# A decoder layer's delta rule and attention: one hop per unit of weights, substitution over both token tiles, bias loaded a step ahead

## The chip, the cores and the metric

One core of one Trainium2 chip runs the whole program. The metric is the device time of one execution in microseconds; the median of three runs is compared. A profile is one further execution, recorded by the hardware profiler.

## The reference, cut to what matters

One decoder layer over 256 tokens of width 2048, in fp32. After an RMS norm, one projection feeds two branches of 8 heads of 128: a gated delta rule (convolution over 4 tokens, chunks with a triangular solve, a state carried from chunk to chunk) and block attention with a relative position bias (256 tokens are one block, so it is plain causal attention). Both are gated, merged and projected; then a SwiGLU network of width 5632.

```python
u = rmsnorm(h); q_a,k_a,v_a,z_a,beta_a,dec_a,q_b,k_b,v_b,gate_a,gate_b = split(u @ w_in)
# delta rule, per head and chunk; L strictly lower triangular
wu = triangular_solve(eye + L, [k*beta*exp(g), v*beta])
v_new = u - w @ S;  o = q_dec @ S + A @ v_new;  S = S*exp(g_last) + k_dec.T @ v_new
y_a = rmsnorm(o, o_norm_w) * silu(z_a)
# attention
y_b = softmax(q_b @ k_b.T * scale + rel_bias, causal) @ v_b
h = h + (sigmoid(gate_a)*(y_a @ w_a) + sigmoid(gate_b)*(y_b @ w_b)) @ w_out
h = h + (silu(u @ w_gate) * (u @ w_up)) @ w_down,  u = rmsnorm(h)
```

## The kernel before, in words

All weights come as 503 *units* of 128x1024 fp32 (512 KB), loaded in order by SP (`Weights.load`, up to 7 raw buffers). ScalarE rounds each to a high part `whi` (line 64), VectorE subtracts to get the low part `wlo` (line 65), up to three units ahead, in 4 buffers each. TensorE multiplies each unit with the activations, themselves split into high and low: `fm_jobs` (lines 156 and 157, 16 matmuls a unit, feature-major output) and `tm_job` (lines 177 to 179, 12 matmuls of 512 columns a unit, token-major output).

Everything else is laid between these units. A *hop* is one call of `tick()`: it runs what stands in `late` (convolution taps, transposes of finished tiles), then goes on with the first generator of `chains` until its next `yield`. `fm_jobs` and `tm_job` call it once for every two units. When a generator ends, the next begins in the same hop. `drain()` ticks without any unit between. The generators are `x_scale` and `beta_decay` (norm of the input, gates of the delta rule; they run beside the first group's projections), `gdn(g)` for two groups of four heads, and `moba(g)` for two groups of heads. `gdn(0)` begins with the second group's convolved projections (24 feature-major units, then 8 for `z`), `gdn(1)` and the `moba`s run beside the attention projections (48 units) and the gated branch products.

In `gdn` a chunk is a *token tile* of 128 tokens, so a group has two tiles. In order: decay (`pgr`, `dec`), transposes of k and q with sums of squares on ScalarE (`ptr`, `junk`), an inverse root on VectorE by shift and three Newton steps (`rr`), the decayed products (`pga`, `mt`), of which the 16x16 diagonal blocks are gathered into `mc`. `mc` is written to DRAM (`dm`) and read back replicated (`lb`, 1024 KB) on ScalarE's DMA queue. The decayed q products (`at`) and GpSimd's masked copies (`ct`) follow. Then VectorE inverts the 16x16 blocks by substitution, 15 steps of a product (line 470) and a sum (line 471) into `X`. The blocks are spread to `E` and the inverse is built up to 32, 64 and 128 rows by transposes and small matmuls (`pD`, `pY`, `pX`, `pE`; lines 499 to 544) in the forms 128x128, 32x32 and 64x64. `solve` and `attend` apply it tile by tile, with the state `S` between; `finish` norms the output (inverse root on VectorE, two multiplications on GpSimd), transposes it (`pyT`) and writes `yaT`.

`moba` scales and transposes q and k (`pqT`), and for each pair of heads loads the bias (256 KB, SP's queue), computes scores `pSc`, softmax into `sc`, transposes (`pPT`) and the product with v (`pO`).

A scheduler lays each engine's instructions into one fixed queue at compile time. What was emitted first goes first unless the scheduler reckons its inputs not ready; an engine then works its queue in order and waits where an input is late. `tc.issue_after(ins)` puts a block behind `ins` in the queue of its engine; the substitution stands behind the last `wlo` that had been emitted. The pools set the rest: tag `t2` has 14 buffers, `aux` (PSUM) 4, `md` 6.

Of the kernel before, what the change touches and what calls it, by code (L numbers as in the profile page):

```python
# [35 lines left out]
TICK = 8  # L36
# [40 lines left out]
def layer(ctx: ExitStack, tc: tile.TileContext, xT, xtok, params, consts, relt, w_bd, w, out):  # L77
# [60 lines left out]

    def drain(left=0):
# [25 lines left out]
    def tm_job(act, nk):  # L165
# [3 lines left out]
        for kc in range(nk):  # L169
# [10 lines left out]
            if kc % (TICK // 2) == TICK // 2 - 1:  # L180
                tick()
# [41 lines left out]
    def x_scale():  # L223
# [7 lines left out]
        yield  # L231
# [35 lines left out]
    def beta_decay():  # L267
# [12 lines left out]
        yield  # L280
# [5 lines left out]
        yield  # L286
# [34 lines left out]
        yield  # L321
        yield
        yield
# [65 lines left out]
    def gdn(g, qk, vT, zw):  # L389
# [3 lines left out]
        for n in range(NT):  # L393
# [7 lines left out]
            dec.append(d)  # L401
        junk = t2("junk")
# [13 lines left out]
        yield  # L416
# [20 lines left out]
        for n in range(NT):  # L437
            m = t2("mt")
            decayed(n, 1, bk2, m)
            mt.append(m)  # L440
            tmp = t2("mtmp")
# [3 lines left out]
            if n == 0:  # L445
                yield
# [8 lines left out]
        yield  # L455
# [7 lines left out]
        yield  # L463
# [25 lines left out]

        yield  # L490
        yield
        yield

        E = []
        for n in range(NT):
            ct = cts[n]
            e = t2("E")
            wide = [P, GH, P // BS, BS]
            nc.vector.tensor_mul(e.rearrange("p h (b i) -> p h b i", i=BS),
                                 X[:, n * GH:(n + 1) * GH].unsqueeze(2).to_broadcast(wide),  # L500
                                 mblk.rearrange("p (b i) -> p b i", i=BS).unsqueeze(1).to_broadcast(wide))
            p = auxt("pD")
            for h in range(GH):
                nc.tensor.transpose(p[:, h], e[:, h], ident)
            d = t2("D")
            nc.scalar.copy(d, p)
            p = auxt("pY")
            for h in range(GH):
                nc.tensor.matmul(p[:, h], ct[:, h], d[:, h], start=True, stop=True)
            y = t2("Y")  # L510
            nc.scalar.copy(y, p)
            p = auxt("pX")
            for h in range(GH):
                nc.tensor.matmul(p[:, h], e[:, h], y[:, h], start=True, stop=True)
            nc.vector.tensor_sub(d, d, p)
            p = auxt("pE")
            for h in range(GH):
                nc.tensor.transpose(p[:, h], d[:, h], ident)
            nc.scalar.copy(e, p)
            w = 32  # L520
            ab = [(slice(o, o + w), slice(o + w, o + 2 * w)) for o in (0, 64)]
            p = auxt("pY")
            y = t2("Y")
            for lo, hi in ab:
                for h in range(GH):
                    nc.tensor.matmul(p[hi, h, :w], mt[n][lo, h, hi], d[lo, h, lo], start=True, stop=True)
                nc.scalar.copy(y[hi, :, :w], p[hi, :, :w])
            p = auxt("pX")
            for lo, hi in ab:
                for h in range(GH):  # L530
                    nc.tensor.matmul(p[hi, h, :w], e[hi, h, hi], y[hi, h, :w], start=True, stop=True)
                    nc.tensor.matmul(p[lo, h, w:2 * w], y[hi, h, :w], e[hi, h, hi], start=True, stop=True)
                nc.vector.tensor_scalar(d[hi, :, lo], p[hi, :, :w], -1.0, None, op0=ALU.mult)
                nc.scalar.mul(e[lo, :, hi], p[lo, :, w:2 * w], -1.0)
            w = 64
            lo, hi = slice(0, w), slice(w, 2 * w)
            p = auxt("pY")
            for h in range(GH):
                nc.tensor.matmul(p[hi, h, :w], mt[n][lo, h, hi], d[lo, h, lo], start=True, stop=True)
            nc.scalar.copy(y[hi, :, :w], p[hi, :, :w])  # L540
            p = auxt("pX")
            for h in range(GH):
                nc.tensor.matmul(p[lo, h, :w], y[hi, h, :w], e[hi, h, hi], start=True, stop=True)
            nc.vector.tensor_scalar(e[lo, :, hi], p[lo, :, :w], -1.0, None, op0=ALU.mult)
            E.append(e)
            yield
# [15 lines left out]
        def finish(n, o):  # L562
            ss = small(f"os{g}{n}", [GH])
            junk = t2("junk")
            for h in range(GH):
                nc.scalar.activation(junk[:, h], o[:, h], AF.Square, accum_out=ss[:, h:h + 1])
            ro = rsqrt(f"or{g}{n}", ss, 1.0 / DH)
            yield
            nc.gpsimd.tensor_mul(o, o, bc(ro, P))
            nc.gpsimd.tensor_mul(o, o, zw[:, n])  # L570
            yield
            p = auxt("pyT")
            for h in range(GH):
                nc.tensor.transpose(p[:, h], o[:, h], ident)
            hi = yaT[:, hs, n * P:(n + 1) * P]
            nc.scalar.copy(hi, p)
            nc.vector.tensor_sub(yaT[:, hs, T + n * P:T + (n + 1) * P], p, hi.bitcast(F32))

        vn0 = solve(0, vs[0])
        p = attend(0, vn0)  # L580
# [6 lines left out]
        nc.scalar.copy(S, p)  # L587
        p = auxt("pkS")
# [11 lines left out]
        yield from finish(0, o0)  # L600
        vn1 = solve(1, rr1)
        p = attend(1, vn1)
# [3 lines left out]
        yield from finish(1, o1)  # L606
# [22 lines left out]
    def moba(g, ssb, raw, vb, ybT):  # L629
# [20 lines left out]
        yield  # L650
        for h in range(0, GH, 2):
            bias = s2.tile([P, 2, T], F32, name="bias", tag="t2", bufs=14)
            nc.sync.dma_start(bias, relt[:, g * GH + h:g * GH + h + 2])
            probs = []
            for i in range(2):
# [18 lines left out]
                probs.append(s)  # L674
            yield
            pO = aux.tile([P, 2, T], F32, name="pO2", tag="aux")
            for i in range(2):
# [5 lines left out]
                nc.scalar.copy(pr, pT[:, :3 * P])  # L683
                nc.tensor.matmul(pO[:, i], vb[:, 0, hh], pr[:, :T], start=True, stop=False)
# [3 lines left out]
            nc.vector.tensor_sub(ybT[:, hs, T:], pO, ybT[:, hs, :T].bitcast(F32))  # L688

# [229 lines left out]
```

## Time and profile before

| what | before |
|---|---|
| median of 3 runs | 1499.94 us (1499.26 to 1501.11) |
| profiled execution | 1498.37 us |
| its span, first to last instruction | 1496.6 us |
| TensorE busy | 1474.1 us, 98% |
| VectorE busy | 868.9 us, 58% |
| ScalarE busy | 675.8 us, 45% |
| GpSimd busy | 56.7 us, 4% |
| weight loads | 503 of 512 KB, median 4.0 us to landing |

The span is what the trace covers; the execution's time has about 1.8 us around it. In the trace's lines PE is TensorE, PEld its weight load, DVE VectorE, ACT ScalarE, POOL GpSimd, SP SyncE. A busy share is a mean over the whole span. Matmuls are pipelined and the ends of their records are modelled, so distances are read from start to start.

### The profile page before, as it was taken

Reading aid. Unit: us, or ns where it says so; the run is one execution under the profiler, and the core shown is the slowest. Engines: PE = TensorE matmul, PEld = TensorE weight load, DVE = VectorE, ACT = ScalarE, POOL = GpSimd, SP = SyncE. Lnnn points to the kernel's source line nnn. Section 1 sums busy time; section 2 is a strip of 40 time slices with the busy share of each in tenths; the row PEclk is TensorE's granted clock in tenths of the full one; section 3 lists DMA queues with packets and bytes.
Section 4 is the critical chain, followed back from the end, with each engine's and each line's share of the span. In section 5 each row is a group of like instructions: output and inputs, shape, how many; then the busy total and the mean of one; then the engine's idle time right before and its main releaser. Section 6 shows DMA issues by size and latency. Waiting matters only on the chain.

```text
span 1496.6 us, 18724 instructions
## 1 busy us (share of the span) xinstructions
PE 1474.1 (98%) x7164; PEld 1227.0 (82%) x7164; DVE 868.9 (58%) x1161; ACT 675.8 (45%) x956; POOL 56.7 (4%) x48
## 2 busy tenths in 40 slices
PE   7999999999999999999999999999999999999998
PEld 6888778887878888888888888888888888888887
DVE  5978957866664445555565555555555555444443
ACT  6645445445454444444554444444444444333332
POOL 0003002301100000000000000000000000000000
PEclk9999999999999999999999999999999999999999
DMA  9564744753546666667666666666666566666661
GB/s 372 168 189 127 209 124 142 191 177 115 181 127 199 195 195 184 187 193 241 192 184 186 194 186 194 184 192 187 196 185 193 186 186 194 194 206 207 194 210 58
DMA packets 77450, 277.82 MB, mean 186 GB/s; under 512 B 8752, under 2 KB 9392, under 8 KB 76976
## 3 DMA queue, kind: packets, MB, share of 16 engines
q1 hardware_dynamic: 75456, 270.46, 59.7%
q10 hardware_dynamic: 1424, 4.59, 1.2%
q0 software_dynamic: 480, 1.57, 0.3%
q8 instruction: 56, 0.92, 0.3%
q14 instruction: 34, 0.28, 0.1%
HBM read 274.36 MB, written 2.23 MB: 185 GB/s over the span
## 4 chain that ended last, share of the span: by engine, by line
PE 91%; DVE 4%; DMA 2%; ACT 1%; issue 1%; POOL 0%; SPq 0%; DVEq 0%; ACTq 0%; POOLq 0%
PE ps L179 27%; PE ps L177 27%; PE ps L178 27%; PE ps L156 3%; PE ps L157 2%; PE pT L189 1%; DVE wlo L65 1%; DMA lb<-dm 1%; DMA bias<-in_relt 1%; DVE cacc L348 1%; DMA wraw<-in_w 0%; ACT whi L64 0%; PE pU L551 0%; PE pO L559 0%; PE pb L279 0%
## 5 line engine op out<-in xcount | busy, mean ns | idle before, releaser
L65 DVE TENSOR_TENSOR wlo<-wraw,whi 128x1024 fp32r<-128x1024 f32 (+1 forms) x505 | 619.9, 1229 | 521.7 <-ACT whi L64 519.7
L64 ACT CAST whi<-wraw 128x1024 fp32r<-128x1024 f32 (+1 forms) x505 | 530.0, 1051 | 680.2 <-PE ps L179 608.0
L177 PE MATMUL ps<-whi,uT 128*128 128x512 f32 x704 | 274.8, 390 | 0.0
L179 PE MATMUL ps<-whi,uT 128*128 128x512 f32 x704 | 273.9, 389 | 0.0
L178 PE MATMUL ps<-wlo,uT 128*128 128x512 f32 x704 | 273.9, 389 | 0.0
L177 PE MATMUL ps<-whi,aT 128*128 128x512 f32 x512 | 202.8, 396 | 0.0
L179 PE MATMUL ps<-whi,aT 128*128 128x512 f32 x512 | 201.3, 393 | 0.0
L178 PE MATMUL ps<-wlo,aT 128*128 128x512 f32 x512 | 200.4, 391 | 0.0
L179 PEld LDWEIGHTS ps<-whi,uT 128*128 128x128 f32 x704 | 132.2, 188 | 27.5
L177 PEld LDWEIGHTS ps<-whi,uT 128*128 128x128 f32 x704 | 132.2, 188 | 27.0
L178 PEld LDWEIGHTS ps<-wlo,uT 128*128 128x128 f32 x704 | 132.2, 188 | 27.0
L156 PE MATMUL ps<-aT,whi 128*128 128x512 f32 x384 | 137.6, 401 | 10.3 <-DVE aT L216 10.2
L179 PEld LDWEIGHTS ps<-whi,aT 128*128 128x128 f32 x512 | 96.2, 188 | 19.7
L177 PE MATMUL ps<-whi,high 128*128 128x512 f32 x288 | 112.0, 389 | 0.0
L178 PE MATMUL ps<-wlo,high 128*128 128x512 f32 x288 | 112.0, 389 | 0.0
L179 PE MATMUL ps<-whi,high 128*128 128x512 f32 x288 | 112.0, 389 | 0.0
L157 PE MATMUL ps<-aT,wlo 128*128 128x256 f32 x384 | 108.6, 283 | 3.1 <-DVE wlo L65 3.1
L178 PEld LDWEIGHTS ps<-wlo,aT 128*128 128x128 f32 x512 | 96.3, 188 | 18.7
L177 PEld LDWEIGHTS ps<-whi,aT 128*128 128x128 f32 x512 | 96.3, 188 | 18.4
L156 PEld LDWEIGHTS ps<-aT,whi 128*128 128x128 f32 x384 | 73.0, 190 | 27.4 <-DVE aT L216 10.2
L157 PEld LDWEIGHTS ps<-aT,wlo 128*128 128x128 f32 x384 | 73.4, 191 | 4.1 <-DVE wlo L65 4.0
L178 PEld LDWEIGHTS ps<-wlo,high 128*128 128x128 f32 x288 | 54.1, 188 | 11.3
(327 smaller groups left out, 1394.3 us busy)
## 6 DMA issues: line engine op xcount, KB each, us to landing
wraw<-in_w SPq DMA_DIRECT2D x503, 512.0 KB, 4.0
xrow<-in_xtok SPq DMA_DIRECT2D x1, 2048.0 KB, 10.2
lb<-dm ACTq DMA_DIRECT2D x2, 1024.0 KB
xr<-in_xtok SPq DMA_DIRECT2D x8, 256.0 KB, 5.5
xc<-in_xT ACTq DMA_DIRECT2D x3, 512.0 KB, 8.1
out<-fo POOLq DMA_DIRECT2D x6, 256.0 KB, 4.4
bias<-in_relt SPq DMA_DIRECT2D x4, 256.0 KB, 4.1
xc<-in_xT ACTq DMA_DIRECT2D x2, 256.0 KB, 5.0
```

Of the source, the lines that this page charges most:

```text
L64: self.last_hi = self.nc.scalar.copy(hi[:, f], raw[:, f])
L65: self.last_lo = self.nc.vector.tensor_sub(lo[:, f], raw[:, f], hi[:, f].bitcast(F32))
L156: nc.tensor.matmul(ps[:, j], hi[:, sl], act[:, kc], start=kc == 0, stop=False)
L157: nc.tensor.matmul(ps[:, j, :T], lo[:, sl], act[:, kc, :T], start=False, stop=kc == nk - 1)
L177: nc.tensor.matmul(ps[:, n], ah, hi[:, sl], start=kc == 0, stop=False)
L178: nc.tensor.matmul(ps[:, n], ah, lo[:, sl], start=False, stop=False)
L179: nc.tensor.matmul(ps[:, n], al, hi[:, sl], start=False, stop=kc == nk - 1)
L189: nc.tensor.transpose(p[:, i], src[:, i * P:(i + 1) * P], ident)
L348: nc.vector.scalar_tensor_tensor(acc[:, j, d:], u[:, j, :T - d], w[:, 3 - d:4 - d], acc[:, j, d:], op0=ALU.mult, op1=ALU.add)
```

## The change

`tick()` is called once for every unit. `rest(n)` yields n times without work. The generators get more `yield`s, so that each hop has about half of what it had. In the diff below, the first `rest(2)` that is shown stands behind the issue of `dm<-mc` and `lb<-dm`. The order inside `gdn` changes in four places: the substitution's 15 steps are cut in five hops, each behind the last `wlo` of its own time; the build-up from 16 to 128 rows is written step by step with both token tiles in each step, where each tile went through all steps in one hop; the transposes of v (`pv`, `vs`) move from before it to its last but one hop; `finish` takes both tiles together after the second `attend`. In `moba` the bias of the first pair is loaded in the first hop, that of the next pair behind the softmax of the one before, and each head has hops of its own.

```diff
-            if k0 % TICK == TICK - 4:
-                tick()
+            tick()
...
-            if kc % (TICK // 2) == TICK // 2 - 1:
+            if kc % 2 == 1:
                 tick()
...
-        yield
+        yield from rest(2)
         for n in range(NT):
             decayed(n, 0, rk, dec[n])
             at.append(dec[n])
+            yield
             ct = t2("ct")
             nc.gpsimd.tensor_mul(ct, mt[n], bcm(mlev, GH))
             cts.append(ct)
             yield
-        yield
...
-        with tc.issue_after(W.last_lo.ins):
-            nc.vector.tensor_copy(X, bcm(eye, NT * GH))
-            for i in range(1, BS):
+        for i in range(1, BS):
+            with tc.issue_after(W.last_lo.ins):
+                if i == 1:
+                    nc.vector.tensor_copy(X, bcm(eye, NT * GH))
                 nc.vector.tensor_mul(prod[:, :, :i + 1], lbv[:, :, i, :i + 1], X[:, :, :i + 1])
                 nc.vector.tensor_reduce(X[:, :, i], prod[:, :, :i + 1], axis=AX.X, op=ALU.add)
-
-        yield
+            if i % 3 == 0:
+                yield
+        E, D, Y = [], [], []
+        for n in range(NT):
...
+            E.append(e)
+        yield
+        for n in range(NT):
+            p = auxt("pD")
...
+            nc.scalar.copy(D[n], p)
+        yield
+        for n in range(NT):
+            p = auxt("pY")
...
+        yield
+        for n in range(NT):
+            p = auxt("pX")
...
+            nc.vector.tensor_sub(D[n], D[n], p)
+        yield
+        for n in range(NT):
+            p = auxt("pE")
...
+            p = auxt("pY")
+            for lo, hi in ab:
...
+        yield
...
-        def finish(n, o):
+        def finish(os):
+            ros = []
+            for n, o in enumerate(os):
...
+                    nc.scalar.activation(junk[:, h], o[:, h], AF.Square, accum_out=ss[:, h:h + 1])
+                ros.append(ss)
+            yield
+            for n, o in enumerate(os):
+                ro = rsqrt(f"or{g}{n}", ros[n], 1.0 / DH)
+                nc.gpsimd.tensor_mul(o, o, bc(ro, P))
+                nc.gpsimd.tensor_mul(o, o, zw[:, n])
+            yield from rest(2)
+            for n, o in enumerate(os):
+                p = auxt("pyT")
...
+        biases = []
+
+        def bias_load(h):
+            if h < GH:
+                biases.append(s2.tile([P, 2, T], F32, name="bias", tag="t2", bufs=14))
+                nc.sync.dma_start(biases[-1], relt[:, g * GH + h:g * GH + h + 2])
+
+        bias_load(0)
         yield
...
-            bias = s2.tile([P, 2, T], F32, name="bias", tag="t2", bufs=14)
-            nc.sync.dma_start(bias, relt[:, g * GH + h:g * GH + h + 2])
+            bias = biases.pop(0)
...
                 probs.append(s)
+                yield
+            bias_load(h + 2)
             yield
```

## Rows read from the trace of the kernel before

**Rows 1.** The page: busy time of each engine, and the group of the splits.

```profile
PE 1474.1 (98%) x7164; PEld 1227.0 (82%) x7164; DVE 868.9 (58%) x1161; ACT 675.8 (45%) x956; POOL 56.7 (4%) x48
...
L65 DVE TENSOR_TENSOR wlo<-wraw,whi 128x1024 fp32r<-128x1024 f32 (+1 forms) x505 | 619.9, 1229 | 521.7 <-ACT whi L64 519.7
```

**Rows 2.** Busy us per engine (instructions), PEclk, DMA share, GB/s: 106.43 to 187.02 us.

```profile
106.43:187.02 80.59, 75.77 (x454) 66.10 (x452) 72.23 (x136) 40.55 (x81) 13.25 (x9) 1.00 0.58 166
```

**Rows 3.** Waits, whole span: us in total, times, longest; five of TensorE, one of VectorE.

```profile
PE ps L156 <- DVE aT L216: 10.2, 1, 10.2
PE ps L157 <- DVE wlo L65: 3.1, 3, 1.5
PE pPT L681 <- DVE sc L672: 1.8, 2, 1.0
PE pD L504 <- DVE E L499: 1.8, 1, 1.8
PE pyT L574 <- POOL o L570: 0.8, 1, 0.8
...
DVE prod L470 <- DMA lb<-dm: 5.2, 2, 3.2
```

**Rows 4.** TensorE's timeline at 577 us: start, us, what [idle before].

```profile
577.04 0.39 PE L179 MATMUL ps<-whi,aT 128*128 128x512 f32 x1
577.27 1.03 PE L189 MATMUL pT<-ident,mixb 128*128 128x128 f32 x8
578.07 0.47 PE L177 MATMUL ps<-whi,aT 128*128 128x512 f32 x1
578.38 0.40 PE L178 MATMUL ps<-wlo,aT 128*128 128x512 f32 x1
```

**Rows 5.** TensorE's timeline at 196 us, a visit of 64x64 matmuls.

```profile
195.87 0.39 PE L177 MATMUL ps<-whi,aT 128*128 128x512 f32 x1
196.19 0.67 PE L539 MATMUL pY<-D,mt 64*64 64x64 f32 x8
196.79 0.50 PE L178 MATMUL ps<-wlo,aT 128*128 128x512 f32 x1
197.13 0.39 PE L179 MATMUL ps<-whi,aT 128*128 128x512 f32 x1
```

**Rows 6.** VectorE's timeline in the first delta rule.

```profile
120.81 0.17 DVE L117 TENSOR_SCALAR rr0x<-ss 128x16 f32<-128x16 f32 x1 [2.41 <-ACT junk L412]
143.25 1.37 DVE L449 TENSOR_TENSOR mc<-mc,cst 128x128 f32<-128x128 f32 x1
159.68 0.22 DVE L468 COPY X<-cst 128x128 f32<-128x128 f32 x1
161.88 0.18 DVE L470 TENSOR_TENSOR prod<-lb,X 128x16 f32<-128x16 f32 x1 [1.98 <-DMA lb<-dm]
185.88 0.67 DVE L499 TENSOR_TENSOR E<-X,cst 128x512 f32<-128x512 f32 x1
```

**Rows 7.** The chain that ended last, 138 to 176 us: start, us, what.

```profile
144.65 2.46 DMA dm<-mc
147.14 14.65 DMA lb<-dm
```

**Rows 8.** VectorE's and TensorE's timeline at the second bias load of `moba(0)`.

```profile
410.07 0.35 DVE L662 SCALAR_TENSOR_TENSOR sc<-pSc,rt,bias 128x128 f32<-128x128 f32 x1 [2.07 <-DMA bias<-in_relt]
411.49 0.39 PE L178 MATMUL ps<-wlo,aT 128*128 128x512 f32 x1
412.75 0.61 PE L681 MATMUL pPT<-ident,sc 128*128 128x128 f32 x3 [0.87 <-DVE sc L672]
```

**Rows 9.** GpSimd's and VectorE's timeline in two finishes.

```profile
361.34 2.19 POOL L570 TENSOR_TENSOR o<-o,zw 128x512 f32<-128x512 f32 x1
375.12 2.04 POOL L638 TENSOR_TENSOR qb<-qb,rt 128x512 f32<-128x512 f32 x2 [4.71 <-DVE or11w L122]
375.27 0.90 DVE L121 TENSOR_TENSOR or11w<-or 128x4 f32<-128x4 f32 x1
```

More of the change, by code (lines that the diff above doesn't have):

```diff
@@ L35 @@
 RAW = 7
-TICK = 8
 class Weights:
@@ L137, in tick, with rest @@
                 chains.pop(0)
+    def rest(n):
+        for _ in range(n):
+            yield
     def drain(left=0):
@@ new lines, in gdn @@
+        yield
+        for n in range(NT):
+            p = auxt("pY")
+            for h in range(GH):
+                nc.tensor.matmul(p[:, h], cts[n][:, h], D[n][:, h], start=True, stop=True)
+            Y.append(t2("Y"))
+            nc.scalar.copy(Y[n], p)
+        yield
+        for n in range(NT):
+            p = auxt("pX")
+            for h in range(GH):
+                nc.tensor.matmul(p[:, h], E[n][:, h], Y[n][:, h], start=True, stop=True)
+            nc.vector.tensor_sub(D[n], D[n], p)
@@ new lines, in gdn @@
+        yield
+        w = 32
+        ab = [(slice(o, o + w), slice(o + w, o + 2 * w)) for o in (0, 64)]
+        for n in range(NT):
+            p = auxt("pE")
+            for h in range(GH):
+                nc.tensor.transpose(p[:, h], D[n][:, h], ident)
+            nc.scalar.copy(E[n], p)
+            p = auxt("pY")
+            for lo, hi in ab:
+                for h in range(GH):
+                    nc.tensor.matmul(p[hi, h, :w], mt[n][lo, h, hi], D[n][lo, h, lo], start=True, stop=True)
+                nc.scalar.copy(Y[n][hi, :, :w], p[hi, :, :w])
@@ new lines, in gdn @@
+        yield
+        for n in range(NT):
+            p = auxt("pX")
+            for lo, hi in ab:
+                for h in range(GH):
+                    nc.tensor.matmul(p[hi, h, :w], E[n][hi, h, hi], Y[n][hi, h, :w], start=True, stop=True)
+                    nc.tensor.matmul(p[lo, h, w:2 * w], Y[n][hi, h, :w], E[n][hi, h, hi], start=True, stop=True)
+                nc.vector.tensor_scalar(D[n][hi, :, lo], p[hi, :, :w], -1.0, None, op0=ALU.mult)
+                nc.scalar.mul(E[n][lo, :, hi], p[lo, :, w:2 * w], -1.0)
@@ L474, in gdn @@
+        yield
+        w = 64
+        lo, hi = slice(0, w), slice(w, 2 * w)
+        for n in range(NT):
+            p = auxt("pY")
+            for h in range(GH):
+                nc.tensor.matmul(p[hi, h, :w], mt[n][lo, h, hi], D[n][lo, h, lo], start=True, stop=True)
+            nc.scalar.copy(Y[n][hi, :, :w], p[hi, :, :w])
         vs = []
@@ L512, in gdn @@
             p = auxt("pX")
             for h in range(GH):
[L514 to L546, printed above, removed]
+                nc.tensor.matmul(p[lo, h, :w], Y[n][hi, h, :w], E[n][hi, h, hi], start=True, stop=True)
@@ L560, in attend @@
             return p
[L562 to L577 removed]
+        def finish(os):
+            ros = []
+            for n, o in enumerate(os):
+                ss = small(f"os{g}{n}", [GH])
+                junk = t2("junk")
+                for h in range(GH):
+                    nc.scalar.activation(junk[:, h], o[:, h], AF.Square, accum_out=ss[:, h:h + 1])
+                ros.append(ss)
+            yield
+            for n, o in enumerate(os):
+                ro = rsqrt(f"or{g}{n}", ros[n], 1.0 / DH)
+                nc.gpsimd.tensor_mul(o, o, bc(ro, P))
+                nc.gpsimd.tensor_mul(o, o, zw[:, n])
+            yield from rest(2)
+            for n, o in enumerate(os):
+                p = auxt("pyT")
+                for h in range(GH):
+                    nc.tensor.transpose(p[:, h], o[:, h], ident)
+                hi = yaT[:, hs, n * P:(n + 1) * P]
+                nc.scalar.copy(hi, p)
+                nc.vector.tensor_sub(yaT[:, hs, T + n * P:T + (n + 1) * P], p, hi.bitcast(F32))
         vn0 = solve(0, vs[0])
+        yield
         p = attend(0, vn0)
@@ L599, in gdn @@
         yield
-        yield from finish(0, o0)
         vn1 = solve(1, rr1)
+        yield
         p = attend(1, vn1)
@@ L605, in gdn @@
         yield
-        yield from finish(1, o1)
+        yield from finish((o0, o1))
     def moba_project(g):
```

46 lines of the change are left out of this document (18 added, 28 removed).

## The prediction

> **What bounds the kernel now.** I read the page's busy table first: TensorE is busy for 1474.1 us, 98% of the span [rows 1]. Busy time can hide stalls, because the ends of matmuls are modelled, so next I read start-to-start distances in the TensorE timeline. In a quiet place one 512-column weight matmul starts 0.23 us after another [rows 4]; twelve of them, one unit of weights, take 2.7 us (a feature-major unit has as many columns). The whole kernel is such a stream, the granted clock is 1.00 where I looked [rows 2], and the change removes no column. What it can win is only time in which TensorE stands still or switches. The list of TensorE's waits has that in five lines [rows 3]: 10.2 us at the start, before the first input is there (the change doesn't reach it), then 3.1 us for the low parts `wlo` in three places, 1.8 us for `E`, 1.8 us for `sc`, 0.8 us for `o`. So 7.5 us lie in code that the change touches. By starts they are dearer: `pPT` is listed with 0.87 us, but it starts 1.26 us after the matmul before it instead of 0.23, so 1.03 are lost [rows 8]. By that ratio of 1.18 the 7.5 us are some 9 us: 3.7 for `wlo`, 2.1 for `E`, 2.2 for `sc`, 1.0 for `o`.
>
> Then the stretch in which most of it falls, 106.4 to 187.0 us, where the first delta rule runs beside the second group's projections: VectorE is busy for 72.2 of 80.6 us there [rows 2], and for most of what is left it waits on something. There VectorE, not TensorE, sets the pace.
>
> **The hops.** A hop per unit instead of per two units doubles the steps, and the generators get about twice the yields: gdn 36 hops in 36 units where it was 20 in 40, moba 16 in 16 where it was 5 in 10. Counted through the loops, the last moba step falls on hop 101 of the 128 there are before the closing `drain()`, and the second delta rule ends on hop 71, before `yaT` is read (from hop 80 on). So no drain gets work that it hadn't. Splitting work over more borders costs TensorE nothing that the rows show: eight transposes at a border take 0.80 us, and 0.08 more on the next weight matmul (0.31 for 0.23), 0.11 each as between themselves [rows 4]. Against that stands a stall at any border at which an input is late; I take 0, with up to 0.1 us (the 0.08) for each of some 40 new groups, 4 us, as the upper end.
>
> **Substitution over both tiles.** A small-tile matmul (32x32, 64x64) between weight matmuls costs more than itself. The stretch from 195.87 to 197.13 holds two weight matmuls (0.46) and eight 64x64 ones [rows 5]; by their group's length these are some 0.06 apart, 0.46 together. 1.26 - 0.92 = 0.34 us is lost entering and leaving. I count 17 such visits in the timeline, two tiles by two groups of heads. Afterwards `pE`/`pY`, `pX`, `pY`, `pX` are each one hop for both tiles: 4 visits a group, 8 in all. 9 x 0.34 = 3.1 us off. Ends: 0, if the visits are broken up again between tiles, and 17 x 0.34 = 5.8. The copies between these steps get a whole unit (2.7 us) to land. SBUF: `mt`, `at`, `ct`, `E`, `D`, `Y` for two tiles and `k0` are 13 of the 14 buffers of `t2`, so no allocation should wait.
>
> **Bias a step ahead.** VectorE waited 2.07 us for the second bias load of a moba group, and TensorE lost 1.03 us at `pPT` behind it [rows 8]; the same happens in the other group (two times, 1.8 us in all [rows 3]). The load now has at least three hops, 8 us, against a wait of 2.07 us now; SP issues it among weight loads that are far ahead. The whole wait goes: 2.2 us off. Next late there is the chain reduce, exponential, reciprocal, scale, which gets a hop for each head. Ends: 0 and 2.2.
>
> **The delta rule's first group, on VectorE.** The sum of VectorE's work up to the end of the stretch hardly changes: same convolutions, splits, substitution; `vs` (two instructions) leaves, the second tile's `E` and the two subtractions into `D` come in. As long as VectorE sets the pace, spreading doesn't shorten anything; only its own idle time counts. That is 2.41 us for the squares before `rr` and 1.98 us for the copy `lb` [rows 6]. The first stays: TensorE's `ptr` now comes in two hops, `rr` a hop later. The second grows. From the end of the addition into `mc` (143.25 + 1.37 = 144.62) the two DMAs take 2.46 and 14.65 us, and the first product starts 17.3 us later [rows 6, 7]. VectorE reached that product at 159.90 (159.68 + 0.22), 15.3 us after the addition. In that time eight units of work stand between the hop that queues the copy and the hop of the first product; from now on six (hop 9 to hop 15). Two splits fewer (a split takes 1.23 us [rows 1]) is 2.5 us, so VectorE comes there after about 12.8 us and waits 4.5 instead of 1.98: 2.5 us more. In a stretch at VectorE's pace that comes through to `wlo` and TensorE. At the end, `E` is made a hop ahead of `pD`, where it came 1.2 us after TensorE needed it (made at 185.88, 0.67 long); but now `pD` needs both tiles' `E` and the next `wlo` stands before them. I leave its 2.1 us at 1.9. Together +2.3. Ends: all of 3.7 + 2.1 = 5.8 us gone, and, if nothing but the six splits (7.4 us) lies between the addition and the product, a wait of 9.9 us, +7.9. Behind the waiting product VectorE holds `wlo` of the next unit, and TensorE waits for that. I take the middle, since the rows show both the pace and the copy's length. In the second group VectorE has room (units of the moba projection); there it waits for `lb` even longer (3.2 us of 5.2 in two waits), and no wait of TensorE answers to it [rows 3].
>
> **Finish.** Both tiles' output norms now run together: two inverse roots on VectorE, four multiplications on GpSimd, then two free hops before `pyT`. GpSimd's second multiplication took 2.19 us and ended at 363.53, and TensorE's `pyT` waited 0.8 us for it [rows 3, 9]. The first tile's work now starts long before, the second's has four units (11 us) from `pO` to `pyT`. I take 0.5 us where it was 1.0: 0.5 off. Ends: 1.0 off, 4 on.
>
> How the second end could come about: while GpSimd multiplied `qb` (375.12 to 377.16), an instruction of the inverse root took 0.90 us [rows 9]; elsewhere one takes 0.17 [rows 6]. The Trainium skill, "SBUF — State Buffer", section "Who interferes with whom", has a rule for it: a VectorE instruction with two SBUF inputs and a GpSimd one that reads SBUF exclude each other for their whole length. This trace agrees (0.90 against 0.17 us). By that rule the second tile's root would run against the first tile's multiplications; it is the last rival below.
>
> **Sum.** -3.1 (visits) - 2.2 (bias) + 2.3 (first group) - 0.5 (finish) + 0 (borders) = -3.5 us. On the profiled execution, 1498.4 us with a span of 1496.6, that gives 1494.9. It ran 1.6 us under the median of the runs, 1499.9; against that median I forecast 1496.4 us.
>
> **Rivals.** Spreading does what it looks like: VectorE's bursts go, `wlo` is never late, `E` is early. For it: the stalls at `wlo` come after runs of other VectorE work. Against it: 72.2 of 80.6 us. With all of it gone -3.1 - 2.2 - 5.8 - 0.5 = -11.6, 1488.3; with half of the 5.8, 1491.2. Chance 0.19.
>
> No change: the scheduler already laid other weight matmuls between the steps of a chain, and small visits break up again (0 instead of -3.1). Then -2.2 + 2.3 - 0.5, about 1499.5. For it: TensorE stands still for so little. Chance 0.21.
>
> Slower, through `lb`: the product's place in VectorE's queue moves two units nearer to a copy that takes 17 us and can't be hurried. At 9.9 us of wait, and both `E` in front of `pD` (2 x 0.67), it is +7.9 + 1.3 - 3.1 - 2.2 - 0.5 = +3.4: 1503.3 and up. It decides from a wait of about 9 us. Against it: the convolution taps of a whole job lie between too. Chance 0.13.
>
> Finish against GpSimd: `pyT` waits 2 us in each group. If each two-input instruction of the second root runs into a multiplication (0.7 us more in some three of them, 2 us), then -3.5 + 0.5 + 4 = +1, about 1501. Chance 0.05.
>
> **How the numbers follow.** The forecast, 1494 to 1499, has 0.42. A measurement of this kernel tells 0.2%, 3 us, from no change: faster is below 1496.9, slower above 1502.9. Faster: 0.27 of the forecast's 0.42, 0.19 of the first rival, 0.01 of the second: 0.47. Slower: 0.13 and 0.02 each of the second and the last: 0.17. Same: 0.36. The range of 1489.5 to 1502.5 leaves out the lower end of the first rival and most of the slower one.
>
> **What would show it.** In the profile after: `sc` waits for no bias, and `pPT` for no `sc`; four visits of small tiles in each group, with both tiles in one place; the wait of `prod` for `lb` in the first group, 4 to 5 us (the forecast), under 2 (the spreading rival) or near 10 (the slower one); the `wlo` waits of TensorE between 106 and 187 us at some 5 to 6 us; `pyT` waiting under 1 us. A VectorE that has gaps in that stretch while `wlo` is on time would prove the step on the first group wrong; so would waits of TensorE at new borders (`pU`, `pO`) of more than 4 us in all.

## The result, and the profile after

The changed kernel takes 1511.27 us (median of 6 runs, 1508.33 to 1513.39) against 1499.90 us for the kernel before (1499.26 to 1501.11): a ratio of 1.0077, 95% interval 1.0067 to 1.0087. It is slower, by 11.4 us, where 3.5 us of gain were forecast; the time lies outside the range. The profiled execution took 1508.33 us with a span of 1506.5 us, 9.9 us over the span before. It is the quickest of the six, so the views below show less than the median's loss.

The page of the changed kernel, busy time of each engine and the group of the splits (answer to [rows 1]):

```profile
PE 1476.6 (98%) x7164; PEld 1231.6 (82%) x7164; DVE 868.9 (58%) x1161; ACT 675.4 (45%) x956; POOL 56.6 (4%) x48
...
L64 DVE TENSOR_TENSOR wlo<-wraw,whi 128x1024 fp32r<-128x1024 f32 (+1 forms) x505 | 623.1, 1235 | 526.1 <-ACT whi L63 525.7
```

Same counts of instructions, 868.9 us on VectorE both times. Nothing was added; work was moved. So I looked for the loss in waits and in the speed of TensorE. The waits of TensorE and VectorE, whole span (us in total, times, longest), against [rows 3]:

```profile
PE ps L159 <- DVE aT L218: 9.6, 1, 9.6
PE pD L490 <- DVE E L482: 6.8, 2, 5.5
PE pyT L590 <- POOL o L585: 6.7, 2, 4.2
PE ps L180 <- DVE wlo L64: 2.2, 1, 2.2
...
DVE prod L473 <- DMA lb<-dm: 8.6, 2, 7.0
```

The wait of `pPT` for `sc` is gone, and so are the three `wlo` waits of [rows 3]. But `pD` waits 6.8 us where it was 1.8, `pyT` 6.7 where it was 0.8, and a `wlo` wait of 2.2 us has come at another place. Without the start that is 15.7 us instead of 7.5, so 8.2 more.

The second part is in the granted clock. Stretches of the changed kernel (us, busy us of each engine with instructions, PEclk, DMA share, GB/s), in pairs: a wait, and what came behind it:

```profile
179.07:184.56 5.49, 0.00 (x1) 0.00 (x1) 5.49 (x15) 3.19 (x5) 0.00 (x0) 0.94 0.55 173
184.56:187.33 2.77, 2.77 (x12) 2.67 (x13) 2.77 (x4) 1.20 (x3) 0.00 (x0) 0.50 0.15 12
240.18:244.39 4.21, 0.00 (x1) 0.00 (x1) 3.63 (x3) 1.17 (x2) 4.02 (x2) 1.00 0.75 226
245.36:248.77 3.41, 3.41 (x11) 2.64 (x10) 1.29 (x2) 0.31 (x1) 1.04 (x1) 0.50 0.33 127
296.74:298.89 2.15, 0.00 (x1) 0.00 (x1) 2.01 (x8) 0.85 (x1) 0.00 (x0) 1.00 0.37 151
299.98:303.39 3.41, 3.41 (x10) 2.63 (x9) 3.41 (x15) 0.27 (x1) 1.55 (x2) 0.50 0.72 217
```

After each of the three waits, TensorE runs at 0.50, 1.2 instead of 2.4 GHz, for 2.77, 3.41 and 3.41 us. (The first fall begins inside the wait, whose row shows 0.94.) What that costs can be read in TensorE's timeline behind the second wait (start, us, what):

```profile
246.56 0.63 PE L179 MATMUL ps<-whi,aT 128*128 128x512 f32 x1
246.99 0.63 PE L180 MATMUL ps<-wlo,aT 128*128 128x512 f32 x1
247.42 0.63 PE L181 MATMUL ps<-whi,aT 128*128 128x512 f32 x1
...
249.20 0.39 PE L180 MATMUL ps<-wlo,aT 128*128 128x512 f32 x1
249.43 0.39 PE L181 MATMUL ps<-whi,aT 128*128 128x512 f32 x1
```

One weight matmul starts 0.43 us after another, then 0.23 again: half of 3.41 us is lost, 1.7 us. With 1.4 us for the first, the three make 4.8 us. So +8.2 (waits) + 4.8 (clock) - 0.6 (the start waits 9.6 instead of 10.2) - 1.5 (visits, below) = +10.9, against 9.9 in the spans; 1.0 us stays unassigned. The busy time of PE rose by only 2.5 us: it hides most of this.

The clock also makes the runs of the changed kernel differ. Its mean over the execution was 0.996 in the run of 1508.33 us, 0.994 in four runs of 1509.67 to 1512.99, 0.993 in that of 1513.39. Between 0.996 and 0.994 lie 0.002 of 1508 us, 3 us: by this estimate the median has some two falls more than the profile shows.

Where the three waits come from. First group (TensorE's and VectorE's timelines, [idle before]):

```profile
184.56 1.12 PE L490 MATMUL pD<-ident,E 128*128 128x128 f32 x4 [5.49 <-DVE E L482]
...
183.83 1.28 DVE L482 TENSOR_TENSOR E<-X,cst 128x512 f32<-128x512 f32 x2
```

`E` is made at 183.83 us, 2 us earlier than in [rows 6], at VectorE's old pace (busy 70.5 of the same 80.6 us, [rows 2] had 72.2). TensorE comes to `pD` at 179.07, 5.8 us earlier than before, when it came there at 184.84 (the matmul started at 186.60 after a wait of 1.76). By the borders `pD` could have moved by two units, from eight behind the hop of the first product to six. It moved by less than one, as the weight matmuls ahead of it show (stretches up to TensorE's arrival, its instructions on `ps` alone, before and after):

```profile
0.00:184.84 184.84, 161.44 (x864) 1.00 0.66 214
0.00:179.07 179.07, 160.22 (x853) 1.00 0.68 216
```

Eleven weight matmuls are 2 us here. The other 3.8 us are waits that TensorE no longer has on its way: 0.6 at the start, and the three `wlo` waits of [rows 3], which all lay in this stretch (kernel before):

```profile
143.38 0.38 PE L157 MATMUL ps<-aT,wlo 128*128 128x256 f32 x1 [0.33 <-DVE wlo L65]
148.77 0.39 PE L157 MATMUL ps<-aT,wlo 128*128 128x256 f32 x1 [1.45 <-DVE wlo L65]
176.34 0.39 PE L157 MATMUL ps<-aT,wlo 128*128 128x256 f32 x1 [1.28 <-DVE wlo L65]
```

So in the first group TensorE waited 4.9 us in four pieces before, with no fall of the clock behind any of them. Now it waits 5.5 us in one piece, with a fall. The waiting was gathered rather than added: +0.6, and 1.4 for the clock. Second group, VectorE:

```profile
288.07 0.21 DVE L472 COPY X<-cst 128x128 f32<-128x128 f32 x1
295.28 0.18 DVE L473 TENSOR_TENSOR prod<-lb,X 128x16 f32<-128x16 f32 x1 [7.00 <-DMA lb<-dm]
```

VectorE stands for 7.0 us at the copy, `wlo` behind it, and TensorE waits 2.15 us for that one. In the first group the same wait is 1.6 us (8.6 less 7.0). And the first finish, GpSimd, then TensorE, then two instructions of the inverse root on VectorE:

```profile
240.23 1.90 POOL L584 TENSOR_TENSOR o<-o,or 128x512 f32<-128x512 f32 x1 [2.36 <-DVE or L122]
242.21 2.13 POOL L585 TENSOR_TENSOR o<-o,room 128x512 f32<-128x512 f32 x1
...
244.39 0.66 PE L590 MATMUL pyT<-ident,o 128*128 128x128 f32 x4 [4.21 <-POOL o L585]
...
235.60 0.91 DVE L120 TENSOR_TENSOR or01w<-or 128x4 f32<-128x4 f32 x1
...
236.74 1.15 DVE L122 SCALAR_TENSOR_TENSOR or<-or01w,or 128x4 f32<-128x4 f32 x1
```

The second tile's `pO` starts at 227.79 us and its `o` is done at 244.34: 16.5 us, for which the changed kernel leaves four units, 11 us. The root of the second tile runs from 233.44 to 240.09 with splits of 1.2 us between its steps, and two of its steps take 0.91 and 1.15 us instead of 0.16 while GpSimd multiplies the first tile (235.45 to 237.87).

The first tile's multiplications come that late because its own root was cut apart. Between two of its steps VectorE does other work for 4.4 us, most of it four instructions on the second group's `zw`, of which the first is shown:

```profile
228.78 0.16 DVE L120 TENSOR_TENSOR or00w<-or 128x4 f32<-128x4 f32 x1
228.86 0.68 DVE L383 SCALAR_TENSOR_TENSOR zw<-zw,ps 128x512 f32<-128x512 f32 x1
...
233.37 0.15 DVE L121 SCALAR_TENSOR_TENSOR or00w<-or00w,or00x 128x4 f32<-128x4 f32 x1
```

### The profile page after: what moved, and what is told of

Read it like the earlier page. It is cut to its first block, busy times and chain, and to the rows that moved or that the text cites. A ratio compares the mean times of both kernels' runs of the same rounds, so it can differ in the third digit from the quotient of the medians.

```text
span 1506.5 us, 18731 instructions
## 1 busy us (share of the span) xinstructions
PE 1476.6 (98%) x7164; PEld 1231.6 (82%) x7164; DVE 868.9 (58%) x1161; ACT 675.4 (45%) x956; POOL 56.6 (4%) x48
## 4 chain that ended last, share of the span: by engine, by line
PE 91%; DVE 4%; DMA 1%; ACT 1%; issue 1%; POOL 1%; SPq 0%; DVEq 0%; ACTq 0%; POOLq 0%
PE ps L179 27%; PE ps L180 27%; PE ps L181 27%; PE ps L159 4%; PE ps L160 2%; DVE wlo L64 2%; PE pT L191 1%; DMA lb<-dm 1%; DVE cacc L348 0%; DVE prod L473 0%; DMA wraw<-in_w 0%; ACT whi L63 0%; DVE X L474 0%; POOL o L585 0%; PE pb L281 0%
```

## The experiments

Ratios are against the kernel before, run beside each (medians 1499.32 to 1499.45 us), with their 95% intervals. My theory then: three results (`lb`, `E`, `o`) are asked for in fewer units than they take, and the falls of the clock follow from those waits. Rivals: VectorE's total work sets the pace wherever the borders stand; the five-hop cut of the substitution or the side-by-side build-up costs time of itself.

**1. pD two hops later** (in the changed kernel, behind the loop that makes `E`).

```
-        yield
+        yield from rest(3)
```

> The changed kernel with two more hops between the making of E and pD (all later steps of gdn two units later). Theory: TensorE stops at pD (5.5 and 1.3 us) because the border follows the substitution by too few units, and each longer stop is followed by a fall of the granted clock to 0.5 for 3.4 us, worth some 1.7 us. Then the pD waits of 6.8 us go under 1 us, one fall goes with them, and the median of 1511.3 us falls by 7 to 10, to 1501 to 1504. Rival: VectorE sets the pace of this stretch, so what doesn't show at pD shows at wlo or at the next border; then the sum of TensorE's waits stays within 2 us of 25.3 (15.7 without the start), and the time within 2 us of 1511.

1509.42 us (1508.53 to 1510.30), ratio 1.0067 [1.0055, 1.0080]: 1.9 us less than the changed kernel. The theory's expectation missed, and the rival's came: without the start the waits still add up to 15.6 us. The second group's wait at `pD` went, but its `wlo` wait grew from 2.2 to 4.5. The first group's `pD` stayed at 5.8 us, and at the same weight matmul, with 853 ahead of it. So the run is no test of more time for `E` there. That the scheduler laid `pD` by its own reckoning of when `E` is ready is my reading and not shown; shown is that a hop only says where a step can't come before.

**2. pyT two hops later** (`finish`).

```
-            yield from rest(2)
+            yield from rest(4)
```

> The changed kernel with four free hops instead of two ahead of pyT in finish. Theory: pyT's wait of 6.7 us (4.2 and 2.5) is only a border that comes two units too early for two inverse roots and four multiplications one after the other. Then it goes under 1 us, a clock fall goes with it, and the time falls by 7 to 10 us, to 1501 to 1504. Rival: GpSimd and VectorE hold each other up for as long as both have work, and work that is put beside them later makes it worse; then the wait falls by no more than 3 us and the time by no more than 4.

1503.39 us (1501.77 to 1505.17), ratio 1.0023 [1.0014, 1.0033]: 7.9 us less. TensorE's waits without the start:

```profile
PE pD L490 <- DVE E L482: 6.3, 2, 5.7
PE ps L180 <- DVE wlo L64: 4.4, 1, 4.4
PE ps L160 <- DVE wlo L64: 0.4, 1, 0.4
```

`pyT` is gone from the list, the fall at 245 us with it. 6.7 us of waits and a fall of 1.7 make 8.4; the `wlo` wait grew from 2.2 to 4.4, so not all of it came back in the profile (6.5 us of span).

**3. X two hops later** (behind the issue of `dm<-mc` and `lb<-dm`).

```
-        yield from rest(2)
+        yield from rest(4)
```

> The changed kernel with four free hops instead of two behind the copies dm and lb, so that the substitution and all behind it come two units later, as many units after the copy as before the change. Theory: VectorE's waits for lb (1.6 and 7.0 us) go to under 3 us in all, and with the second the wlo wait of 2.2 us and one clock fall: 3 to 5 us off, 1506 to 1508; pD's wait stays at 5 to 7 us, because its border moves along with the substitution. Rival: the copy is the root of pD's wait too; then pD's wait falls under 3 us and the time by 8 or more.

1502.98 us (1498.43 to 1504.37), ratio 1.0019 [1.0010, 1.0028]: 8.3 us less, more than the 3 to 5 expected. TensorE's waits without the start, and VectorE's at the copy:

```profile
PE pyT L590 <- POOL o L585: 4.7, 2, 2.6
PE pD L490 <- DVE E L482: 4.5, 2, 4.2
PE ps L160 <- DVE wlo L64: 0.4, 1, 0.4
...
DVE prod L473 <- DMA lb<-dm: 3.1, 2, 1.8
```

The wait at the copy fell from 8.6 to 3.1 us, and not only the `wlo` wait behind it: `pyT` and `pD` each gave back 2 us too, and only two falls of the clock are left. The 2 us at `pyT` are not the copy's. Run 1 has the same 4.7 us there, with 9.1 us at the copy. What runs 1 and 3 share is that the first group's finish comes two units later: the `zw` instructions then stand ahead of the first tile's root, and the second tile's chain from `pO` to `o` takes 14.5 us in both instead of 16.5. Of the 1.3 us at the first group's `pD` little can be the copy's either, whose wait there went from 1.6 to 1.3 only.

**4. The kernel before with the bias load alone.**

```
+        bias_load(0)
...
-            bias = s2.tile([P, 2, T], F32, name="bias", tag="t2", bufs=14)
-            nc.sync.dma_start(bias, relt[:, g * GH + h:g * GH + h + 2])
+            bias = biases.pop(0)
...
+            bias_load(h + 2)
```

> The kernel before with the bias load alone moved ahead as in the change (first pair in moba's first hop, next pair behind the softmax). Theory: the two waits of pPT for sc (1.8 us by the list, 2.2 by starts) go and nothing else changes: 2 us faster, 1497.7. Rival: the wait at pPT is the softmax chain and not the bias; then sc's wait for the bias goes, pPT still waits over 1 us, and the time stays within 1 us.

1496.83 us (1495.50 to 1497.88), ratio 0.9984 [0.9975, 0.9993]: faster than both kernels, by 2.6 us against the one before, where the prediction's term was 2.2. The other waits stay as they were, and the clock doesn't fall before the last work:

```profile
PE ps L157 <- DVE wlo L65: 3.4, 3, 1.7
PE pD L504 <- DVE E L499: 1.8, 1, 1.8
PE pyT L574 <- POOL o L570: 0.8, 1, 0.8
```

So all that is lost is in the rest of the change, which costs some 14 us (11.4 and 2.6, each against the kernel before as run beside it).

**5. X and pyT both two hops later** (edits 2 and 3 together).

> The changed kernel with both moves that helped one by one: the substitution two hops later, and pyT two hops later again. Theory (each wait of TensorE stands by itself, and the falls of the clock with them): the waits that are left are pD's, 4.2 us in the first group with one clock fall; pyT's 4.7 us and the second fall go. 5 to 8 us faster than with the substitution alone moved (1503.0): 1495 to 1498. Rival: VectorE's or GpSimd's lateness only moves on; then the time is within 2 us of 1503.

1499.80 us (1498.31 to 1500.69), ratio 1.0002 [0.9993, 1.0010]: 11.5 us less than the changed kernel, but some 2 us over what I expected. The miss has a place (stretches, columns as above):

```profile
318.00:325.75 7.75, 7.75 (x47) 6.79 (x45) 2.45 (x2) 3.96 (x6) 0.00 (x0) 1.00 0.72 220
325.75:333.09 7.34, 6.04 (x118) 5.21 (x117) 3.29 (x6) 3.98 (x10) 0.00 (x0) 1.00 0.34 113
333.09:343.33 10.24, 10.24 (x59) 8.21 (x57) 2.52 (x5) 2.22 (x6) 0.00 (x0) 0.50 0.01 2
```

From 325.75 to 338.1 us TensorE has no weight matmul at all: the last five hops of the second group's build-up stand in one heap ahead of one weight matmul (the first of unit 96, counted in the timeline), with short waits between them, 1.3 us in all. Inside it the clock falls for 10.24 us, with no wait over 0.6 us in the heap before that. Every run of this kernel shows a mean clock of 0.995. Pushing hops back had pushed this build-up late, six hops behind where the changed kernel has it.

**6. pD four hops later** (`rest(5)` for `yield` in the changed kernel).

> The changed kernel with four more hops between E and pD (two more left pD in the same place of TensorE's queue, 179.2 us, and its wait at 5.8 us). Theory now: the scheduler had put pD two units behind its border by its own reckoning, and VectorE is later than reckoned by 5.5 us there; a border two units further on (5.5 us) covers it. Then pD's wait in the first group falls under 1.5 us and a clock fall of 7 us with it: 1511 less 7 to 9, 1502 to 1504. Rival: VectorE sets the pace, the lateness shows at wlo or further back; pD's wait falls but other waits of the first group take its place, time within 2 us of 1509.

1507.67 us (1502.21 to 1512.29), ratio 1.0060 [1.0042, 1.0077]. `pD`'s wait is down to 0.9 us and the fall at 184 us is gone, but eight hops more for the two groups make the same heap at 327.7 us, with waits at `pY` (2.9), `wlo` (2.7), `pyT` (2.6), `pU` (1.9) and falls of 3.41 and 6.83 us. The forecast of 1502 to 1504 missed: a wait was traded for others, as the rival has it. Here the clock separates the runs most widely: the one at a mean clock of 1.000 took 1502.21 us, those at 0.995 and 0.996 took 1506.43 to 1508.64, those at 0.993 took 1510.51 and 1512.29. By that one run this kernel is some 3 us behind the kernel before even without a fall.

**7. The substitution in one hop**, the five hops kept empty behind it.

```
-        for i in range(1, BS):
-            with tc.issue_after(W.last_lo.ins):
-                if i == 1:
-                    nc.vector.tensor_copy(X, bcm(eye, NT * GH))
+        with tc.issue_after(W.last_lo.ins):
+            nc.vector.tensor_copy(X, bcm(eye, NT * GH))
+            for i in range(1, BS):
...
+        yield from rest(5)
```

> The changed kernel with the substitution in one hop again, behind one wlo, and the four other hops empty, so all other steps stay where they are. If cutting the substitution in five is what makes E late (each fifth stands behind a wlo of its own, and E behind the last), then E is ready 5 us earlier or more, pD's wait falls under 1.5 us, and wlo waits of 1 to 4 us come back: 1503 to 1508. If VectorE's total work and the copy decide, E is late as before (4 to 6 us), and the time is within 2 us of 1511.

1511.41 us (1509.44 to 1512.92), ratio 1.0081 [1.0068, 1.0094], as the changed kernel. Cutting the substitution in five is neither the loss nor a gain.

**8. Finish tile by tile**, at the same last hop: the first tile's norm and multiplications run under the second tile's solve.

```
+        f0, f1 = finish(0, o0), finish(1, o1)
+        next(f0)
         yield
         vn1 = solve(1, rr1)
...
-        yield from finish((o0, o1))
+        next(f1)
```

> The changed kernel with the output norm by tile again: the first tile's squares and root beside the second solve, its multiplications beside the second attend, and the second tile's in the hops behind; pyT of the second tile on the same hop as in the change, of the first one hop earlier. If running both tiles' roots and multiplications together is what makes pyT wait (6.7 us), the wait falls under 2 us and the time by 5 to 9 us, to 1502 to 1506. If the four units from pO to pyT are too few for one tile too, the second tile's wait stays at 1.5 to 4 us a group, and the time falls by less than 4.

1506.86 us (1505.60 to 1508.13), ratio 1.0052 [1.0040, 1.0064]. `pyT` waits 3.6 us instead of 6.7 (1.5 and 2.1 a group, as the second expectation has it; the 4.4 us of time lie between the two). About half of that wait was due to both tiles' finishes together, half to four units being too few for one.

**9 and 10. The first group's finish beside the second group.** Both kernels are run 5 with the second group begun earlier: `finish` of the first group goes on in the second group's first hops. Run 9 has, besides, `pD` two hops later in the first group.

```
-        yield from finish((o0, o1))
+        if g == 0:
+            tails.append(finish((o0, o1)))
+        else:
+            yield from finish((o0, o1))
...
+    def beside(chain):
+        for _ in chain:
+            for tail in tails:
+                next(tail, None)
+            yield
...
-        chains.append(gdn(g, qk, vT, zw))
+        chains.append(gdn(g, qk, vT, zw) if g == 0 else beside(gdn(g, qk, vT, zw)))
```

```
-        yield
+        yield from rest(3 if g == 0 else 1)
```

> The same as the run with the tail beside and pD later, but pD stays where the changed kernel has it. All work is done. Theory: the heap at unit 96 and the fall of the clock at 333 us go, pD's wait of about 4 us in the first group and the fall behind it stay: 1495 to 1498 us, 4 to 6 us above the run with pD later. Rival (the heap isn't due to the second group's late beginning): the fall near 333 us stays, 1499 to 1500 us.

> The changed kernel with both X and pyT two hops later, and two more edits: the finish of the first group no longer stands in the chain ahead of the second group, its hops run beside the second group's first hops, so that the second group begins six hops earlier than in the run with X and pyT later (L390 of its first hop at unit 68 instead of 72, with the next edit counted); and in the first group pD comes two hops later. All work is done. Theory (the loss is three producers given too few units, and the fall of the clock at 333 us came because the second group, begun late, had five hops' matmuls placed in one heap ahead of the first weight matmul of unit 96): no heap at unit 96 and no fall near 333 us, pD's wait of 4.2 us below 1, pyT none, lb about 2; 4.2 + 1.7 us come back for pD and some 3 for the heap, against the 1499.8 us of the run with X and pyT later: 1491 to 1495 us, below the 1496.8 us of the kernel before with the bias alone ahead. Rival (side by side with cut substitution costs of itself, by more visits and by queues that fill at every border): 1497 to 1500 us with waits of several short kinds.

Run 10: 1497.63 us (1496.49 to 1498.67), ratio 0.9987 [0.9979, 0.9996]. The heap is gone, and so is the fall at 333 us; the same 25 us in run 10:

```profile
320.00:345.00 25.00, 25.00 (x232) 19.95 (x231) 10.53 (x16) 11.29 (x20) 0.00 (x0) 1.00 0.37 121
```

So the heap came from the second group's late beginning. Removing heap and fall gained 2.2 us net: an earlier second group waits 5.7 us at the copy where it waited 1.6, and the fall at the first `pD` lasts 6.83 us instead of 3.41. Why the scheduler can't let that build-up pass unit 96 was not tried. Run 9: 1496.31 us (1495.21 to 1498.02), ratio 0.9981 [0.9972, 0.9990], 1.3 us better, not the 4 to 6 expected: `pD` was laid at the same weight matmul as in run 10 (877 ahead of it in both), as in run 1, and waits on:

```profile
PE pD L496 <- DVE E L488: 4.1, 1, 4.1
PE ps L185 <- ACT vb L653: 0.8, 1, 0.8
PE ps L166 <- DVE wlo L64: 0.5, 1, 0.5
PE ps L186 <- DVE wlo L64: 0.2, 1, 0.2
```

**11. The same, tile by tile**: run 9 with the build-up of the kernel before, one tile after the other (three hops each), and the transposes of v ahead of both.

```
-        for n in range(NT):
-            p = auxt("pD")
-            for h in range(GH):
-                nc.tensor.transpose(p[:, h], E[n][:, h], ident)
-            D.append(t2("D"))
-            nc.scalar.copy(D[n], p)
-        yield
...
+        for n in range(NT):
+            ct, e = cts[n], E[n]
+            p = auxt("pD")
...
+            yield from rest(3)
```

> The run with the tail beside and pD later, but the build-up of the inverse (pD to the second pX) is done tile after tile as in the kernel before, tile 0 in one hop and tile 1 three hops later, with the transposes of v ahead of both; the hops in all are the same. All work is done. Theory: side by side saves TensorE visits of the 32- and 64-row tiles, 17 to 14 with 1.5 us of them in the profile of the changed kernel: the tile-by-tile form is 1 to 3 us slower than the run it is made from, 1493 to 1497 us, with pY, pX and pE waits below 1 us each. Rival (the larger number of pending evictions at each border of the side-by-side form costs what the visits save): within 1 us or faster.

1495.08 us (1494.03 to 1498.10), ratio 0.9974 [0.9964, 0.9983]. Not slower than run 9; the theory missed here, the rival stands. It is the best of all kernels by its median, though its interval meets those of runs 4, 9, 10 and 12. Its runs at a mean clock of 1.000 took 1494.03 to 1494.96 us, at 0.999 1495.08 to 1496.56, at 0.997 (the profiled one) 1498.10. Not every kernel is ordered so: run 12 took 1495.03 and 1495.70 us at 1.000, and 1494.85 to 1497.54 at 0.998.

**12. The first group's X early again**: run 11 with X of the first group two hops earlier and `pD` at the same place.

```
-        yield from rest(4)
+        yield from rest(2 if g == 0 else 4)
...
-        yield from rest(3 if g == 0 else 1)
+        yield from rest(5 if g == 0 else 1)
```

> The tile-by-tile run, but in the first group X begins two hops earlier, where the changed kernel has it, and E's hop rests two longer, so that pD and all behind it keep their units. All work is done. Theory (in the first group pD is late because VectorE gets to X late, not because of the unit pD is given): pD's wait of 1.5 us and the wait of 2.8 us behind it go below 1 us in sum, the fall of the clock behind them goes with them, and the lb wait of the first group is 1 to 2 us: 1492 to 1494.5 us. Rival (VectorE is held by its own total of work in that stretch, wherever X begins): pD's wait stays over 1 us, 1495 to 1496 us.

1495.55 us (1494.85 to 1497.56), ratio 0.9977 [0.9967, 0.9986]: no gain over run 11. Half of the mechanism came as the theory has it, the time as the rival has it:

```profile
PE pY L518 <- ACT D L515: 2.5, 1, 2.5
PE ps L186 <- DVE wlo L64: 2.0, 2, 1.7
...
DVE prod L479 <- DMA lb<-dm: 4.8, 2, 2.9
```

`pD` (1.5 us in run 11) waits no more, nor does the clock fall in this profile. But `pY` behind it still waits 2.5 us (2.8 in run 11), and a `wlo` wait of 1.7 us has come just ahead of `pD`, at 187.21. It isn't the copy: the first group's product waits 1.9 us for it here and waited 2.3 in run 11. The wait of TensorE changed its place, as the rival has it.

## Why the prediction was wrong

By place, in the profiles, waits and clock together: finishes +7.6 us, second group +5.2, first group +2.0, bias -1.8, visits -1.5, start -0.6. The forecast had -0.5, 0, +2.3, -2.2, -3.1 and 0. So the steps that failed are the finish, the second group put at nothing, and the clock.

**Finish, -0.5: wrong sign, +5.9 and 1.7 of clock, the step that failed worst.** "The second's has four units (11 us)" was set against nothing: the chain from `pO` to the last multiplication wasn't added up. It took 16.5 us: subtraction and square, seven microseconds of root between splits, 4.1 us of GpSimd. Run 2 gives 7.9 us back. The two steps of 0.91 and 1.15 us beside GpSimd's multiplications cost under 2 us of the 6.7, and run 8 shows that half of the wait is there with the tiles apart. These two steps bear out the Trainium skill, "SBUF — State Buffer", section "Who interferes with whom": a two-input VectorE instruction and a GpSimd one that reads SBUF hold each other up. The last rival had the place and 2 us a group; it was 4.2 and 2.5. That the first finish would meet the second group's `zw` on VectorE was in no rival; by runs 1 and 3, where it does not, it is some 2 us of the first wait.

**"In the second group VectorE has room": put at nothing, +3.5 and 1.7 of clock.** The row behind it, a wait of 3.2 us that no wait of TensorE answered to, showed how much room there was; I read it as no limit. At 7.0 us the room was used up: `wlo` came 2.15 us late and the clock fell, and `pD` waited 1.3 us. Run 3 gives 8.3 us back, but it moved X in both groups. In its profile (6.9 us less span) 4.3 us come from the second group's `wlo` and `pD` waits and their fall, 3.8 from the first finish and its fall, and 1.7 are lost again to a fall at the second finish. The rival through `lb` had the mechanism and a deciding point of some 9 us, but in the first group.

**The clock, not in the sum at all: 4.8 us in the profile**, counted above with the three places, and more in five of the six runs. [Rows 2] said 1.00, and I took it to hold after the change as well.

**First group, +2.3: nearly the right size, by luck.** The forecast took two splits out from between the addition and the first product. None went: VectorE's timeline has six there in both kernels, it reached the product at 159.95 as before, and `lb` waited 1.6 us, not 4.5. No `wlo` was late in this stretch, as the spreading rival has it; all the waiting stood at `pD`. The failed step here is "I leave its 2.1 us at 1.9": the 15 steps ahead of `E` take VectorE 21 to 22 us in either kernel, and a TensorE that no `wlo` stops comes to `pD` that much earlier and waits 5.5 us there. "VectorE, not TensorE, sets the pace" fits all kernels: in 13 of the 14 profiles TensorE's waits between 140 and 200 us add up to 4.4 to 6.1 us, at `wlo`, `pD`, `pY` or `pE`, wherever the borders stood (run 6: 3.2). What sets that sum was not tested.

**Visits, -3.1: mis-sized, with no gain left in the end.** (It is the build-up that became side by side; the 15 substitution steps took both tiles before as well.) Each group was to have four visits of small tiles; there are seven, because the scheduler lays weight matmuls between the two tiles' `pE`/`pY` pieces. More important, 0.34 us isn't the price of a visit. By starts, with 27 ns for each 32x32 matmul and 58 for each 64x64 one, a visit that held `pX` of 32 rows, with `pY` or without, cost 0.07 to 0.14 us before; side by side `pY` is a visit by itself and costs 0.35. Those with `pE` or with 64x64 matmuls cost 0.30 to 0.67 in both. By this reckoning the 17 cost some 5.4 us before, the 14 some 3.9 after: 1.5 us off, half of the term. Run 11 against run 9 shows no gain of the side-by-side form in the time.

**Bias, -2.2: right.** Run 4 measured 2.6 (1.0 to 3.7 by its interval).

**Borders, 0: right for eight transposes at a border, and no wait at `pU` or `pO` came in the changed kernel.**

Of the signs named beforehand, "four visits" failed (seven), "`pyT` waiting under 1 us" failed (6.7), "`wlo` waits at 5 to 6 us between 106 and 187 us" failed (none), and the wait of `prod` for `lb` of 1.6 us was the spreading rival's sign, not the forecast's. "No bias wait" held. The sign that would prove the step on the first group wrong came: no `wlo` was late there while VectorE stood idle for 10.1 of 80.6 us, where it had been 8.4.

## What to carry to other kernels

When steps are spread by a count of borders, each producer's own length (a copy of 17 us, a norm of 16.5) has to be set against the time between its border and that of whoever reads it, in units, for every pair and in every group, with whatever other work its engine has there; halving the hop halves that time where the number of hops isn't doubled. Where a step really stands is read from the trace: a border is only a lower bound. A wait of 2 us on the engine that sets the end can cost 4, because the clock falls behind it, so one long wait can be dearer than several short ones of the same sum. And before pushing a late step back, see what may run beside it instead: hops that were added ahead of the second group came back as a heap in it.

## What the runs showed of the hardware that was not expected

In the changed kernel's profile the granted clock fell to 0.50 in or behind TensorE's waits of 5.5, 4.2 and 2.15 us, each time for 3.41 us, while waits of 0.3 to 1.8 us in the kernel before and in run 4 left it at 1.00. Near 2.5 us it goes either way: the changed kernel's second `pyT` waited 2.53 us (376.01) with no fall behind it, the same wait in runs 3 and 7 (2.56 and 2.55 us) had one, and in run 12 a wait of 2.5 us had none. That can be some of the difference between runs of one kernel, but no run shows it. And the clock fell without a long wait, for 10.24 us, in the heap of run 5, where TensorE was busy for 6.04 of 7.34 us, most of its matmuls 32x32 or 64x64.

The Trainium skill, "TensorE: Matmul & The Clock Gate", tells of two such cases. In its section "HAM oscillation — how this bites in real kernels" TensorE waits for data between bursts of matmuls, in "A second HAM failure mode: psum-queue depth-cycling" it idles shortly but often between groups of them, and both times the clock falls again and again. The falls here agree with the first, though a single wait is enough. The heap of run 5 has short gaps as in the second (0.27 to 0.59 us), but whether they or the small matmuls let the clock fall is not shown.
